# Transposed and split queries and keys made in the projection stage of a decoder-layer step on one Trainium2 core

## The chip, the core and the metric

The kernel runs on one core of a Trainium2 chip. A core has five engines that each work through a queue of their own, strictly in order: TensorE (PE: matmuls and transposes; PEld is its loading of the stationary operand), VectorE (DVE), ScalarE (ACT), GpSimd (POOL) and SyncE (SP, which here only issues DMAs). DMAs move data between the device memory and the core's SBUF; PE writes its results to PSUM banks, from which DVE and ACT read them. An instruction that waits for a semaphore holds up everything behind it on its engine. The metric is device time in microseconds (us) of one execution, lower is better.

## What is computed

One layer of a decoder for a prompt of 1024 rows and a decode batch of 8 rows that share the weights. Cut to what matters here:

```python
h = rmsnorm(x) @ w_in                      # q, k, v (8 heads of 64), f, u, z
logf = log_sigmoid(f + b_f)
# prompt, per head, causal:
c = cumsum(logf)
s = q @ k.T * 64 ** -0.5 + c[:, None] - c[None, :]
att = softmax(mask(s)) @ v
# decode rows: the same, against 8192 cached positions per row
x = x + concat(rmsnorm(att), rmsnorm(u * mixed(z))) @ w_o
x = x + cross_attention(x, 256 memory rows)
x = x + conv_gated_mlp(x)
return rmsnorm(x), k, v, logf, ...
```

Everything is fp32. A product is made from split operands: a value is written as a high part (rounded to the matmul's fp32r form) and a low part (the remainder), and three matmuls add high*high, high*low and low*high. `split` does this: ACT copies the high part, DVE subtracts it from the source to get the low part.

## The kernel before

**The prompt's stages** follow each other on PE: the projection by w_in (about 0 to 235 us of the profile, called p1 here), the attention of rows 0 to 511 (hf = 0, to about 355 us, mixed with the memory's keys and values), the attention of rows 512 to 1023 (hf = 1, to about 495 us), then w_o, cross-attention and the MLP of each half.

**p1** goes through five column groups: Q, then O_F (forget logits and u), K, V, Z. Each has 8 tiles of 128 rows, and a tile is 24 matmuls of 512 columns (48 of 260 in O_F). The first four Q tiles are computed together (`by_rows`). The weights come as four pieces per group on SP (L249), and each is split by ACT (wh, L235) and DVE (wl, L236). `evac` (L467) takes a tile out of PSUM with ACT (L469) and stores it with a DMA that ACT issues (L470): q to the scratch tensor q_d, k and v to the outputs.

**The decode batch** runs as a background program between the prompt's pieces. How many of its steps are issued is paced by the `yield` values of the prompt's code (table PACE): a stage with fewer or smaller yields gets fewer steps. A step on the cached keys multiplies a gathered 1 MB tile with the queries on DVE (L1444, 128x2048 in p1) and reduces it on DVE (L1448); within the attention the same work is cut into 128x512 pieces (L1435, L1436). GpSimd issues the gathers (L1428 keys, L1489 values), PE sums the values (L1495). The queries for this come by SP: `qs_d` is stored (L465) and read back as a broadcast row (L1398, tile d). Later the decode rows go through w_o, w_cq, the cached memory keys (cmk: L1680 multiplies, L1682 reduces, 16 pieces of each), whose scores PE transposes at L1687, the memory values, and the MLP.

**The attention** works per pair of heads (hp = 0 to 3). `load` fetches the pair's q, k and v from device memory in rows. `setup` makes the operands of the score matmuls: PE transposes four blocks of q (L750) and of k (L779); ACT copies the high parts of both heads (L757, L784, 64x512 each), DVE subtracts the low parts (L774, L788, 64x512 each), GpSimd copies the high part a second time (L758 for q, L785 for k), and GpSimd's DMAs add four rows that carry the cumulated logits. For hf = 0 GpSimd stores the finished k operands in ks_d (L791, L792); for hf = 1 SP reads them back (L769, L770) and only the second 512 keys are made anew. Then come for each block of 128 queries: scores on PE (L807, L809, L811), the row maximum on DVE (L813, L816), the exponential on ACT (L814, L817), transposes of the result on PE (L836), their copies by ACT or DVE (L843, L841), and the products with v on PE (L852). The setup of the next pair is run between the score blocks of the present one, at the places that LD and ST name.

**The order**: the code is written in the order of the stages, and a scheduler then puts each engine's instructions into one fixed queue, by its own estimate of when each could start. So a change in one place moves instructions of other parts in the queues; on the chip the queue is followed in order, whatever the true times are. Tiles come from rotating pools: `T2` has NT buffers of 128x512, `BA`, `BB` and `MS` are PSUM banks.

Of the kernel before, what the change touches and what calls it, by code (L numbers as in the profile page):

```python
# [7 lines left out]
F32 = mybir.dt.float32  # L8
# [52 lines left out]
LD = [(0, 1, 0), (0, 0, 0)]  # L61
ST = [(0, 1, 1), (0, 1, 1)]
# [5 lines left out]
NT = 7  # L68
# [3 lines left out]
SB = 2  # L72
# [6 lines left out]
def build(nc, tc, ctx, a, phases=None):  # L79
# [123 lines left out]
    q_d = dram.tile([T, AW], F32, tag="q_d", name="q_d")  # L203
# [6 lines left out]
    ks_d = dram.tile([NH, 64, 2, 512], F32, tag="ks_d", name="ks_d")  # L210
# [163 lines left out]
    def p1(early):  # L374
# [125 lines left out]
        for tt in range(8):  # L500
            ps, ps2 = BK(), BK()
            mm_chunk(tt, ws, ps[:, 0:260], 0, 260)
            mm_chunk(tt, ws, ps2[:, 0:260], 260, 260)
            if tt == SD - 1:
# [44 lines left out]
        for c0, dst in ((O_K, k_d), (O_V, v_d)):  # L549
            ws, sps = loaded(c0, 512, [(0, 512)])  # L550
            for tt in range(8):
                ps = BK()
                mm_chunk(tt, ws, ps, 0, 512)
                if tt == SD - 1:
# [15 lines left out]
                evac(ps, dst, rstd, tt)  # L570
# [155 lines left out]
    def attention(hf, queue, late=None, at=3):  # L726
# [3 lines left out]
        def load(hp):  # L730
            cs = slice(hp * P, (hp + 1) * P)
            qn = tpool.tile([P, 512], F32, tag="qn", bufs=1, name=nm("qn")).rearrange("p (i c) -> p i c", c=P)
            nc.sync.dma_start(qn, q_d[hf * 512 : (hf + 1) * 512, cs].rearrange("(i p) c -> p i c", p=P))
            if hf == 0:
                kvn = U([P, 2 * nk, P])
                kn, vn = kvn[:, :nk, :], kvn[:, nk:, :]
            else:
                kn, vn = T2().rearrange("p (i c) -> p i c", c=P), U([P, nk, P])
            nc.sync.dma_start(kn, k_d[hf * 512 : nk * P, cs].rearrange("(i p) c -> p i c", p=P))
            nc.sync.dma_start(vn, v_d[: nk * P, cs].rearrange("(i p) c -> p i c", p=P))  # L740
            return qn, kn, vn

        def setup(hp, qn, kn, vn):


            calm = lambda: tc.issue_after(lastexp[0]) if lastexp else nullcontext()
            with behind(ENG.PE):
                tr = BB() if hf else (MS, BB, BA)[SB]()
                for i in range(4):
                    nc.tensor.transpose(tr[:, i * P : (i + 1) * P], qn[:, i, :], ident)  # L750
            qab, ka, kb = [], [], []
            for j in range(2):
                h = hp * 2 + j
                rows = slice(64 * j, 64 * j + 64)
                qq = U([P, 2, 512], F32R)
                with calm():
# [1278 lines left out]
```

## Time and profile before

| | |
|---|---|
| three runs | 1790.96, 1792.46, 1794.57 us; median 1792.46 us |
| the profiled execution | 1791.7 us span, inside the range of the three runs |
| PE, DVE, ACT, POOL busy | 97%, 78%, 41%, 27% of the span |
| mean TensorE clock granted | 0.993 of full speed |
| DMA | 521.06 MB, 291 GB/s mean |

The profile has a page for the whole span and views for any stretch: windows (busy time of each engine), waits (who waited for whom), the timeline (one row per instruction or run of equal ones), the chain (the work that ended last, followed back) and the instructions of one line of the kernel. A row of the timeline gives start and duration in us, engine, line, operation, tiles, and in brackets how long the engine had been idle and what ended that. PE's matmuls are pipelined: one of 512 columns is shown with 0.39 us, and the next starts 0.23 us after it.

### The profile page before, as it was taken

The page shows a single profiled execution, that of the slowest core. Times are in us where ns is not written, and L with a number is a line of the kernel's source. Part 1 is how long each engine was busy: PE and PEld are TensorE (multiplying, and loading weights), DVE is VectorE, ACT ScalarE, POOL GpSimd, SP SyncE. Part 2 cuts the span into 40 slices and gives each one's busy share as a digit, 9 for nine tenths or more (in the row PEclk, how much of TensorE's full clock was granted, in tenths as well). Part 3 has the DMA queues.
Part 4 walks back from the last instruction along what each step waited for, and adds up shares of the span by engine and source line. Part 5 has one row for each costly group of instructions (what it writes and reads, how often), then busy time and mean ns, then how long its engine had stood idle before and what let it go on. Part 6 is the DMA issues. An engine that isn't in the chain of part 4 may idle for free.

```text
span 1791.7 us, 25124 instructions
## 1 busy us (share of the span) xinstructions
PE 1735.9 (97%) x9653; PEld 1285.7 (72%) x9653; DVE 1399.9 (78%) x1733; ACT 733.5 (41%) x1374; POOL 488.3 (27%) x461
## 2 busy tenths in 40 slices
PE   8999999889999999999999999999999999999997
PEld 5787777655677666767777777766666778768875
DVE  4689658989788986989999999898885549855344
ACT  6332355566643635333333244335353233333232
POOL 1252234443222332333322223433322112102110
PEclk9999999999999999999999999999999999999999
DMA  8786798777697975779788788988879587568982
GB/s 291 297 304 226 294 334 319 259 264 244 254 403 279 363 299 224 282 285 345 290 301 313 291 317 311 376 306 346 320 280 350 214 306 249 191 260 297 359 310 80
DMA packets 157074, 521.06 MB, mean 291 GB/s; under 512 B 20874, under 2 KB 40842, under 8 KB 124186
## 3 DMA queue, kind: packets, MB, share of 16 engines
q0 software_dynamic: 57168, 341.14, 50.0%
q1 hardware_dynamic: 92874, 165.73, 26.5%
q10 hardware_dynamic: 6912, 12.59, 1.9%
q8 instruction: 76, 1.25, 0.3%
q14 instruction: 44, 0.36, 0.1%
HBM read 495.47 MB, written 23.93 MB: 290 GB/s over the span
## 4 chain that ended last, share of the span: by engine, by line
PE 53%; issue 9%; DMA 8%; DVE 6%; ACT 2%; POOL 2%; POOLq 0%; DVEq 0%; ACTq 0%; SPq 0%
DMA kv<-cache_v,io 6%; PE ba L272 6%; PE ba L274 6%; PE ba L273 6%; PE dv L1495 4%; PE bb L272 3%; PE bb L273 3%; PE bb L274 3%; PE ba L1063 1%; DVE s L1448 1%; PE ba L1064 1%; PE ba L1065 1%; PE dv L331 1%; DMA kv<-cache_k,io 1%; PE dv L1774 1%
## 5 line engine op out<-in xcount | busy, mean ns | idle before, releaser
L235 ACT ACTIVATE wh<-wr 128x1024 fp32r<-128x1024 f32 (+2 forms) x220 | 228.6, 1044 | 443.3 <-PE ba L273 142.3
L236 DVE TENSOR_TENSOR wl<-wr,wh 128x1024 fp32r<-128x1024 f32 (+2 forms) x220 | 262.7, 1200 | 165.1 <-PE ba L274 57.4
L1428 POOL DMA_INDIRECT kv<-cache_k,io x128 | 186.9, 1460 | 606.8 <-DVE s L1448 327.2
L1444 DVE TENSOR_TENSOR kv<-kv,d 128x1024 f32<-128x1024 f32 (+1 forms) x156 | 258.0, 1681 | 32.6 <-DMA kv<-cache_k,io 32.6
L1448 DVE TENSOR_REDUCE s<-kv 128x16 f32<-128x1024 f32 (+1 forms) x156 | 258.4, 1672 | 0.0
L1489 POOL DMA_INDIRECT kv<-cache_v,io x128 | 160.8, 1256 | 239.4 <-PE dv L1495 155.2
L272 PE MATMUL ba<-u,wh 128*128 128x512 f32 x528 | 209.3, 397 | 0.0
L274 PE MATMUL ba<-u,wl 128*128 128x512 f32 x528 | 209.0, 396 | 0.0
L273 PE MATMUL ba<-u,wh 128*128 128x512 f32 x528 | 208.5, 395 | 0.5 <-DVE u L239 0.5
L272 PE MATMUL ba<-wh,u 128*128 128x512 f32 (+1 forms) x495 | 186.1, 379 | 0.9 <-ACT u L235 0.9
L273 PE MATMUL ba<-wl,u 128*128 128x512 f32 (+1 forms) x495 | 185.1, 375 | 1.3 <-DVE wl L236 1.3
L274 PE MATMUL ba<-wh,u 128*128 128x512 f32 (+1 forms) x495 | 183.4, 375 | 0.0
L1495 PE MATMUL dv<-kv,s 128*32 128x512 f32 x1024 | 127.1, 598 | 1.6 <-DMA kv<-cache_v,io 1.6
L274 PEld LDWEIGHTS ba<-u,wl 128*128 128x128 f32 x528 | 99.2, 188 | 29.0 <-issue 6.5
L272 PEld LDWEIGHTS ba<-u,wh 128*128 128x128 f32 x528 | 99.3, 188 | 26.4 <-issue 4.8
L273 PEld LDWEIGHTS ba<-u,wh 128*128 128x128 f32 x528 | 99.2, 188 | 25.2 <-issue 2.3
L272 PEld LDWEIGHTS ba<-wh,u 128*128 128x128 f32 x495 | 93.0, 188 | 25.0 <-issue 6.5
L272 PE MATMUL bb<-u,wh 128*128 128x512 f32 x272 | 108.7, 400 | 0.0
L274 PE MATMUL bb<-u,wl 128*128 128x512 f32 x272 | 108.0, 398 | 0.0
L273 PE MATMUL bb<-u,wh 128*128 128x512 f32 x272 | 107.9, 397 | 0.0
L273 PEld LDWEIGHTS ba<-wl,u 128*128 128x128 f32 x495 | 93.0, 188 | 20.1 <-DVE wl L236 1.9
L274 PEld LDWEIGHTS ba<-wh,u 128*128 128x128 f32 x495 | 92.9, 188 | 19.5 <-issue 1.6
(454 smaller groups left out, 3310.6 us busy)
## 6 DMA issues: line engine op xcount, KB each, us to landing
wr<-w_up SPq DMA_DIRECT2D x88, 512.0 KB
kv<-w_up POOLq DMA_DIRECT2D x22, 1024.0 KB
wr<-w_down SPq DMA_DIRECT2D x40, 512.0 KB
kv<-w_down POOLq DMA_DIRECT2D x11, 1024.0 KB
wr<-w_in SPq DMA_DIRECT2D x16, 512.0 KB
wr<-w_o SPq DMA_DIRECT2D x16, 512.0 KB
wr<-w_cq SPq DMA_DIRECT2D x16, 512.0 KB
wr<-w_co SPq DMA_DIRECT2D x16, 512.0 KB
```

Of the source, the lines that this page charges most:

```text
L235: nc.scalar.activation(h, src, AF.Copy)
L236: nc.vector.tensor_tensor(l, src, h.bitcast(F32), op=ALU.subtract)
L272: mmul(out, sh, mh, start=(i == 0), stop=False)
L273: mmul(out, sh, ml, start=False, stop=False)
L274: mmul(out, sl, mh, start=False, stop=(i == n - 1))
L331: mmul(ps[32 * j : 32 * j + 32, :w], xT[:, k, :] if nk == 8 else xT[:, k * 8 : k * 8 + 32], raw[:, q, j * w : (j + 1) * w], start=(k == 0) ...
L1063: mmul(pss[i], mh[k][:, tb], wh, start=(k == korder[0]), stop=False)
L1428: nc.gpsimd.indirect_dma_start(kv, None, a["cache_k"], off(kidx[:, b, ch : ch + 1]))
L1444: nc.vector.tensor_tensor(kvv[:, i : i + m, :], kvv[:, i : i + m, :], qb.unsqueeze(1).broadcast_to((P, m, 512)), op=ALU.mult)
L1448: nc.vector.tensor_reduce(s[:, ch * 4 + i : ch * 4 + i + m, :].rearrange("p k h -> p (k h)"), kvv[:, i : i + m, :].rearrange("p k (h d) -> ...
L1489: nc.gpsimd.indirect_dma_start(kv, None, a["cache_v"], off(kidx[:, b, ch : ch + 1]))
L1495: mmul(dv[32 * j : 32 * j + 32, :], s[:, ch * 4 : ch * 4 + 4, :].rearrange("p k h -> p (k h)"), kvv[:, j, :], start=(ch == 1), stop=(ch == ...
```

## The change

The queries and keys are transposed and split once, in p1, right behind the tile that makes them. `evac` hands its tile on, q is no longer stored in rows (q_d is gone), and each Q and K tile is put on a list, `flat`. `turn_over` takes entries from the list between later tiles: two after each of the Q tiles 4 to 7, one after each tile of O_F, K and V as long as there are any. An entry, `operand`, is four PE transposes, one split of 128x512 on ACT and DVE, and four DMAs of 128 KB that SP issues, to qt_d or kt_d (device memory, one 128x1024 block per head: 64 rows high part, 64 rows low part).

In the attention, `load` fetches the finished operands: v, qq (both parts in one transfer), ka and kb, on SP; GpSimd still copies the high parts a second time and still issues the DMAs for the logit rows. `setup` is gone with its transposes, copies and subtractions, and so are ks_d, its stores and re-loads, and the yields in between. NT goes from 7 to 8, and for hf = 1 the next pair is loaded one place later.

```diff
-LD = [(0, 1, 0), (0, 0, 0)]
-ST = [(0, 1, 1), (0, 1, 1)]
+LD = [(0, 1, 0), (0, 1, 0)]
-NT = 7
+NT = 8
         def evac(ps, dst, sc, tt):
             t = T2()
             nc.scalar.activation(t, ps, AF.Copy, scale=sc[:, tt : tt + 1])
-            nc.scalar.dma_start(dst[tt * P : (tt + 1) * P, :], t)
+            if dst is not None:
+                nc.scalar.dma_start(dst[tt * P : (tt + 1) * P, :], t)
+            return t
+        def operand(t, dst, tt):
+            tr = BK()
+            for hp in range(4):
+                nc.tensor.transpose(tr[:, hp * P : (hp + 1) * P], t[:, hp * P : (hp + 1) * P], ident)
+            h, l = T2(512, F32R), T2(512, F32R)
+            split(tr, h, l)
+            d = dst.rearrange("(hp j) (r d) t -> j r d hp t", j=2, r=2)
+            for r, src in enumerate((h, l)):
+                for j in range(2):
+                    nc.sync.dma_start(
+                        d[j, r][:, :, tt * P : (tt + 1) * P],
+                        src[64 * j : 64 * j + 64, :].bitcast(F32).rearrange("d (hp t) -> d hp t", t=P),
+                    )
+        def turn_over(n):
+            for _ in range(min(n, len(flat))):
+                flat.pop(0)()
                 mm_chunk(tt, ws, ps, 0, 512)
+                turn_over(2)
-            evac(ps, q_d, rstd8, tt)
+            flat.append(partial(operand, evac(ps, None, rstd8, tt), qt_d, tt))
...
-                with calm():
-                    nc.scalar.activation(qq[0:64, 0, :], tr[rows, :], AF.Copy)
+                nc.sync.dma_start(qq[:, 0, :].bitcast(F32), qt_d[h, :, s])
                 nc.gpsimd.tensor_copy(qq[0:64, 1, :], qq[0:64, 0, :].bitcast(F32))
...
+                nc.sync.dma_start(ka[j][0:64, :].bitcast(F32), kt_d[h, 0:64, : nk * P])
+                nc.gpsimd.tensor_copy(ka[j][64:128, :], ka[j][0:64, :].bitcast(F32))
+                nc.sync.dma_start(kb[j][0:64, :].bitcast(F32), kt_d[h, 64:128, : nk * P])
                 nc.gpsimd.dma_start(kb[j][64:68, :], ck_d[h, :, : nk * P])
...
                         if hp < 3 and (blk, j, ii) == LD[hf]:
-                            raw = load(hp + 1)
-                        if hp < 3 and (blk, j, ii) == ST[hf]:
-                            nxt = setup(hp + 1, *raw)
-                        if nxt:
-                            next(nxt, None)
-                            yield 1
+                            nxt = load(hp + 1)
```

Counted over the queues: PE's number of transposes and matmuls is the same (64 transposes leave the attention, 64 enter p1). ACT loses 32 copies of 64x512 and gets 16 of 128x512, and loses 8 DMA issues; it gets two more table loads. DVE loses 32 subtractions of 64x512 and gets 16 of 128x512. Of the 64 decode pieces of each kind in the attention (L1435, L1436) 12 move to later stages, where they run as larger ones. GpSimd loses 16 DMAs; its copies of k become 8 of 64x512 and 8 of 64x1024. SP issues 484 DMAs instead of 412: 8 loads of q rows, 8 of k rows and 24 of ks_d leave, 64 stores and 48 loads of the finished operands come.

The queues show where things moved. First DVE's queue where Q ends and O_F begins. Before, the four low parts of O_F's weights (wl, L236) stand ahead of the decode's first multiplications (L1444):

```order
L236 TENSOR_TENSOR wl_556<-wr_554,wh_557 128x1040
L236 TENSOR_TENSOR wl_566<-wr_564,wh_567 128x1040
L236 TENSOR_TENSOR wl_576<-wr_574,wh_577 128x1040
L236 TENSOR_TENSOR wl_586<-wr_584,wh_587 128x1040
L1444 TENSOR_TENSOR kv_348<-kv_348,d_61_345 128x2048
L1444 TENSOR_TENSOR kv_388<-kv_388,d_61_345 128x2048
L1444 TENSOR_TENSOR kv_453<-kv_453,d_61_345 128x2048
L1444 TENSOR_TENSOR kv_485<-kv_485,d_61_345 128x2048
```

In the changed kernel (its own line numbers: L234 is the subtraction of `split` and `wload`, L1419 and L1423 the decode's multiplication and reduction, L1383 a scan of the decode's logits; t are low parts of Q tiles) the same place reads, behind the low parts of Q tiles 0 to 3 and two multiplications:

```order
L1419 TENSOR_TENSOR kv_475<-kv_475,d_61_345 128x2048
L1419 TENSOR_TENSOR kv_532<-kv_532,d_61_345 128x2048
L1383 SCALAR_TENSOR_TENSOR d_157_1173<-rmask,d_157_1173 128x512
L1423 TENSOR_REDUCE s_347<-kv_348 128x32
L234 TENSOR_TENSOR t_90_569<-bb_563,t_89_568 128x512
L234 TENSOR_TENSOR t_93_582<-ba_576,t_92_581 128x512
L1423 TENSOR_REDUCE s_347<-kv_388 128x32
L234 TENSOR_TENSOR wl_639<-wr_637,wh_640 128x1040
L1423 TENSOR_REDUCE s_347<-kv_475 128x32
L234 TENSOR_TENSOR wl_649<-wr_647,wh_650 128x1040
L1383 SCALAR_TENSOR_TENSOR d_451_2679<-rmask,d_451_2679 128x512
L1423 TENSOR_REDUCE s_347<-kv_532 128x32
```

Behind these stand the third and fourth wl and the low parts of Q tiles 6 and 7. So all four multiplications, four reductions, two scans and the low parts of two Q tiles now stand ahead of O_F's last two low parts, of which before none did.

The second place is DVE's queue at the second setup of hf = 1. Before, between the row maxima (L816) and the decode's pieces (L1435, L1436):

```order
L774 TENSOR_TENSOR u_3543<-bb_3538,u_3543 64x512
L774 TENSOR_TENSOR u_3553<-bb_3538,u_3553 64x512
L1435 TENSOR_TENSOR kv_3527<-kv_3527,d_490_2860 128x512
L816 TENSOR_REDUCE mx_3668<-ba_3669 128x1
L1436 TENSOR_REDUCE s_2862<-kv_3527 128x8
L788 TENSOR_TENSOR u_3548<-bb_3595,u_3547 64x512
L788 TENSOR_TENSOR u_3558<-bb_3595,u_3557 64x512
L1435 TENSOR_TENSOR kv_3527<-kv_3527,d_490_2860 128x512
```

In the changed kernel (L803 is the row maximum, L1410 and L1411 the decode's pieces, L861 the scaling of the result) there are no subtractions:

```order
L1411 TENSOR_REDUCE s_3300<-kv_3557 128x8
L932 TENSOR_SCALAR u_2630<-u_2630,rar_3686 128x512
L803 TENSOR_REDUCE mx_3719<-ba_3720 128x1
L803 TENSOR_REDUCE mx_3766<-ba_3767 128x1
L861 TENSOR_TENSOR u_3701<-bb_3703,rl_3671 128x128 x2
L1410 TENSOR_TENSOR kv_3756<-kv_3756,d_615_3298 128x512
L850 RECIPROCAL rl_3820<-ls_3621 128x4
```

What moved here: the four subtractions are gone, and the maxima stand closer together.

The third place is the decode's stage on the cached memory keys, late in the program. Before, between the third and the fourth tile's multiplications (L1680) DVE's queue has six rows of the prompt's MLP, of which these end the stretch (L1307, L1308, L1310: convolution of a tile; L236: low part of a weight piece):

```order
L1682 TENSOR_REDUCE sS_12084<-kv_12246 128x4 x2
L236 TENSOR_TENSOR wl_12530<-wr_12528,wh_12531 128x1024
L1308 SCALAR_TENSOR_TENSOR t_2277_12283<-ba_12258,gp,t_2277_12283 128x510
L1310 TENSOR_TENSOR t_2277_12283<-t_2277_12283,fix_11178 128x2
L1680 TENSOR_TENSOR kv_12293<-kv_12293,d_2278_12289 128x2x512
L1680 TENSOR_TENSOR kv_12293<-kv_12293,d_2279_12290 128x2x512
```

In the changed kernel (L1655 and L1657 are those lines, L1282 the first part of the convolution) the fourth tile follows the third at once:

```order
L1655 TENSOR_TENSOR kv_12305<-kv_12305,d_2295_12301 128x2x512
L234 TENSOR_TENSOR wl_12585<-wr_12583,wh_12586 128x1024
L1655 TENSOR_TENSOR kv_12305<-kv_12305,d_2296_12302 128x2x512
L1655 TENSOR_TENSOR kv_12393<-kv_12393,d_2308_12389 128x2x512
L1657 TENSOR_REDUCE sS_12163<-kv_12215 128x4 x2
L1282 SCALAR_TENSOR_TENSOR t_2317_12436<-bb_12411,gp,t_2317_12436 128x511
L1655 TENSOR_TENSOR kv_12393<-kv_12393,d_2309_12390 128x2x512
```

What moved: the decode reaches this stage later and leaves it at the same point of the prompt. From the first multiplication to the last reduction DVE's queue has 72 rows before and 59 now, and PE's queue has 369 matmuls before and 287 now from the end of the decode's w_cq to L1687.

More of the change, by code (lines that the diff above doesn't have):

```diff
@@ L553, in p1 @@
                 mm_chunk(tt, ws, ps, 0, 512)
+                turn_over(1)
                 if tt == SD - 1:
@@ L731, in load @@
             cs = slice(hp * P, (hp + 1) * P)
[L732 to L739, printed above, removed]
-            nc.sync.dma_start(vn, v_d[: nk * P, cs].rearrange("(i p) c -> p i c", p=P))
[L741 to L750, printed above, removed]
+            vn = U([P, nk, P])
+            nc.sync.dma_start(vn, v_d[: nk * P, cs].rearrange("(i p) c -> p i c", p=P))
             qab, ka, kb = [], [], []
```

52 lines of the change are left out of this document (12 added, 40 removed).

## The prediction

> **What bounds the kernel now.** I read the page first, then the windows, then single stretches.
>
> ```profile
> span 1791.7 us, 25124 instructions
> PE 1735.9 (97%) x9653; PEld 1285.7 (72%) x9653; DVE 1399.9 (78%) x1733; ACT 733.5 (41%) x1374; POOL 488.3 (27%) x461
> ```
>
> TensorE (PE) is busy 97% of the span, and the change leaves its number of transposes and matmuls as it is. So the change cannot save PE work; it can only move it and change how long PE waits. The windows (start and end, length, then busy us of PE, PEld, DVE, ACT, POOL, granted clock, DMA share, GB/s) say where that could be:
>
> ```profile
> 25.00:50.00 25.00, 25.00 (x107) 19.43 (x106) 5.03 (x11) 16.05 (x28) 9.29 (x10) 1.00 0.98 381
> 50.00:75.00 25.00, 22.15 (x154) 17.84 (x153) 13.35 (x8) 9.92 (x13) 0.86 (x1) 1.00 0.84 315
> 75.00:100.00 25.00, 25.00 (x205) 24.15 (x204) 25.00 (x19) 5.95 (x11) 9.08 (x6) 1.00 0.68 251
> 350.00:375.00 25.00, 21.11 (x128) 14.69 (x125) 21.93 (x46) 18.08 (x52) 12.91 (x19) 0.80 0.81 264
> 375.00:400.00 25.00, 21.66 (x150) 14.48 (x148) 20.33 (x33) 15.53 (x36) 9.76 (x12) 0.99 0.66 211
> 400.00:425.00 25.00, 22.06 (x152) 14.06 (x150) 24.88 (x42) 15.53 (x31) 8.22 (x10) 1.00 0.69 239
> 500.00:600.00 100.00, 100.00 (x527) 77.31 (x525) 88.42 (x115) 40.15 (x84) 28.34 (x23) 1.00 0.91 342
> 1480.00:1550.00 70.00, 69.08 (x301) 55.87 (x300) 69.14 (x86) 25.66 (x43) 11.72 (x19) 1.00 0.71 241
> ```
>
> In the projection (p1) PE is full from 75 us on: what is added there, or held up there, is paid. In the attention (350 to 425) PE idles 3 to 4 us of each 25, DVE is 80 to 99% busy, and the clock dips once. From 500 on PE is full again, and at 1480 to 1550 PE and DVE are full together.
>
> **Term 1: p1, +26 us.** The added transposes are cheap. The rows of L750 give one; four follow each other in 0.45 us on the chain:
>
> ```profile
> L750 PE MATMUL bb<-cp,qn x16: 272/273/476, 357.5 to 444.0; 128*128 128x128 f32 x16
> 385.86 0.45 PE bb L750 x4
> ```
>
> 64 transposes are 16 x 0.45 = 7.2 us, half of them for Q and half for K. Their splits (16 on ACT, 16 on DVE) lie beside PE. What costs is DVE's order where Q ends and O_F begins. Its timeline before, and three of PE's rows there:
>
> ```profile
> 53.19 1.24 DVE L236 TENSOR_TENSOR wl<-wr,wh 128x1040 fp32r<-128x1040 f32 x1 [7.73 <-PE ba L273]
> 62.79 3.74 DVE L236 TENSOR_TENSOR wl<-wr,wh 128x1040 fp32r<-128x1040 f32 x3 [8.36 <-ACT wh L235]
> 66.45 8.89 DVE L1444 TENSOR_TENSOR kv<-kv,d 128x2048 f32<-128x2048 f32 x4
> 75.39 1.21 DVE L1408 TENSOR_TENSOR_SCAN d<-rmask,d 128x512 f32<-128x512 f32 x1
> 76.52 8.84 DVE L1448 TENSOR_REDUCE s<-kv 128x32 f32<-128x2048 f32 x4
> 62.25 0.39 PE L272 MATMUL ba<-wh,u 128*128 128x260 f32 x1
> 64.09 0.39 PE L273 MATMUL ba<-wl,u 128*128 128x260 f32 x1 [0.72 <-DVE wl L236]
> 66.58 0.39 PE L273 MATMUL ba<-wl,u 128*128 128x260 f32 x1 [0.35 <-DVE wl L236]
> ```
>
> PE starts O_F at 62.25 and takes each low weight part within half a microsecond of its making; the last one is ready at 66.5. In the changed queue the decode's four multiplications, its four reductions, two scans and two low parts of Q tiles stand ahead of that last part. The multiplications need the broadcast queries d, whose load SP issues late:
>
> ```profile
> 61.45 0.34 SPq L1398 DMA_DIRECT2D d<-qs_d  x1
> SPq L1398 <- DMA qs_d<-t: 23.3, 1, 23.3
> L236 DVE TENSOR_TENSOR u<-ba,u x10: 658/682/692, 617.8 to 1274.5; 128x512 fp32r<-128x512 f32 x10
> ```
>
> That load waited 23.3 us for the store of qs_d, behind weights on busy DMA engines. Without the q_d stores it may go a few us earlier. I let DVE start multiplying at 62.5 (bounds 60 and 66.5, the latter since the old DVE found it ready). Then 8.89 + 2 x 1.21 + 8.84 + 2 x 0.68 + four wl of 1.24 = 26.5 us, and the last wl is ready at 89.0 instead of 66.5: PE is 22.5 us late. 28 of the Q transposes lie inside this wait. The K transposes and the last four (36 x 0.11 = 4.0 us) come on top, since PE is full. Sum +26, between +20 (some of it caught up) and +30. The weights of K wait on SP behind Q's stores, but PE needs them only about 50 us after their old issue at 62.4, so this costs nothing unless the stores take longer than that.
>
> **Term 2: the attention, -24 us.** What vanishes there, per setup: eight transposes, four copies and four subtractions.
>
> ```profile
> L757 ACT ACTIVATE u<-bb x8: 587/592/597, 358.5 to 444.9; 64x512 fp32r<-64x512 f32 x8
> L774 DVE TENSOR_TENSOR u<-bb,u x8: 683/689/696, 361.5 to 446.8; 64x512 fp32r<-64x512 f32 x8
> L1435 DVE TENSOR_TENSOR kv<-kv,d x64: 656/681/1059, 269.9 to 493.0; 128x512 f32<-128x512 f32 x64
> 346.14 0.25 PE ba L750 x3
> 347.67 0.60 ACT u L757
> 396.67 0.59 DVE u L788
> 397.27 0.69 DVE u L788
> 397.96 0.60 DVE kv L1435
> 443.80 0.44 PE bb L750 x4
> ```
>
> The last six are pieces of the chain of waits. From 338 to 495 the chain holds 24 pieces of setup, first and last shown, that add up to 8.4 us, and 5.5 us of decode pieces (L1435, L1436), of which I count half, 2.8, as 12 of 64 move away. For hf = 0 32 transposes (3.5 us) leave a PE that is nearly full. That is 14.7 us directly. DVE is also relieved as a whole: 32 x 0.689 + 12 x (0.681 + 0.68) = 38 us less between 235 and 495, and ACT 32 x 0.59 = 19 us less. If the stretch shrank with DVE's work, it would lose 38 us. The lower bound is 7 us (PE's own transposes). Where DVE's queue is full, as at 400 to 425 (24.88 of 25), every maximum behind a subtraction gets earlier, so I go above the direct sum, to 24.
>
> The 12 pieces are three whole decode steps. They run later, in stages like 500 to 600, where PE has 100.00 of 100 and DVE 88.42: DVE has room for them beside PE, so 0. If it has none, they cost 3 x (2.2 + 2.2) = 13 us (by the rows of L1444 and L1448 above).
>
> GpSimd's second copies stay. Those of 64x1024 are not in the trace; between 0.61 (one of 64x512) and twice that I take 1.2 us.
>
> ```profile
> L758 POOL CAST u<-u x16: 600/624/1712, 241.4 to 449.1; 64x512 fp32r<-64x512 f32 x16
> POOL kv L1428 <- DVE s L1436: 44.5, 6, 16.1
> ```
>
> They stand in GpSimd's queue among gathers that wait up to 16.1 us for DVE, but are issued a pair ahead instead of just in time; I take 0, and 16 us for a handover at which this fails. One copy took 1.71 us instead of 0.60. [...]
>
> **Term 3: the cached memory keys, +7 us.** The decode reaches this stage later and leaves it at the same place in the prompt: PE's queue has 82 matmuls fewer in it, about 19 us at 0.23 us each (107 in 25 us, from 25 to 50). The 32 DVE operations of the stage stay:
>
> ```profile
> L1680 DVE TENSOR_TENSOR kv<-kv,d x16: 1212/1218/1224, 1479.9 to 1539.7; 128x1024 f32<-128x1024 f32 x16
> L1682 DVE TENSOR_REDUCE sS<-kv x16: 1204/1208/1220, 1485.1 to 1545.6; 128x4 f32<-128x1024 f32 x16
> ```
>
> Before, 69.1 us of each engine lie in 70. After, PE has 69 - 19 = 50 us, and DVE, which loses 13 of 72 rows of about half a microsecond, 62.6. PE's transpose at L1687 needs all of it, so PE waits up to 12.5 us; part of it can be made up by DVE rows that run later. I take 7, between 0 and 12.5.
>
> **Sum:** 26 - 24 + 7 = +9 on the profiled 1791.7 us, 1800.7. The median of the runs is 0.8 above this span, so 1801.5; I say 1801.
>
> **Rivals.**
> (a) *The wait in p1 does not arise* (DVE finds the decode's data early, or PE has other work): then p1 costs its transposes alone, 7 or 8 us, and 8 - 24 + 7 = -9 gives 1783.5 on the scale of the runs, faster. Against it: PE's and DVE's queues are fixed, and d was issued at 61.45. Chance 0.1.
> (b) *The attention shrinks with DVE's whole relief*: 26 - 38 + 5 = -7, 1785.5, faster. For it: DVE's 24.88 of 25. Against it: most of the chain there is PE's own. [...] Chance 0.17.
> (c) *The attention gives back only PE's transposes*, since the loop of scores, maximum, exponential and transposes closes behind the gap, or GpSimd's copies are late: 26 - 7 + 7 = +26, 1818.5, slower still. Chance 0.13.
> The forecast has 0.6, with a range of its own from 1794 to 1809.
>
> A difference of 0.2% (3.6 us) is about what a measurement of this kernel can tell from none. Slower by more: 0.52 of the forecast's 0.6 and all of (c), 0.65. Faster: most of (a) and (b), 0.2. Between: 0.15. The range from 1784 to 1817 cuts the outer parts of (a), (b) and (c).
>
> **What would show it.** Right: PE idle for some 20 us between 55 and 90 with "DVE wl" as releaser, the decode's multiplications ahead of it on DVE, and p1 ending about 26 us later; the attention shorter by 20 to 30 us, without setup on the chain; PE waiting at L1687 late in the span. Wrong: PE full from 62 us on; the attention as long as before, with GpSimd's copies or SP's loads as releasers of the scores; or PE waiting in later stages for the moved decode steps.

## The result, and the profile after

The changed kernel takes 1834.97 us (median of 4 runs, 1833.58 to 1836.37), the kernel before, on the same chip, 1791.71 us (4 runs). The ratio is 1.0224, with a 95% interval of 1.0201 to 1.0247: 43 us slower. The forecast said slower, by 9 us.

The page of the changed kernel (span, then busy us of each engine):

```profile
span 1833.6 us, 25147 instructions
PE 1751.0 (95%) x9653; PEld 1295.0 (71%) x9653; DVE 1387.9 (76%) x1703; ACT 727.5 (40%) x1360; POOL 470.5 (26%) x445
```

PE has the same 9653 instructions. The span grew by 41.9 us: PE idles 26.8 us more, and is busy 15.1 us more for the same work; the mean granted clock is 0.982 (0.993 before). DVE, ACT and POOL all have less to do. The windows of the changed kernel (columns as in the prediction; the seventh number is the granted clock) show where:

```profile
50.00:75.00 25.00, 15.74 (x93) 11.68 (x91) 14.66 (x10) 9.38 (x12) 1.56 (x2) 0.86 0.78 231
75.00:100.00 25.00, 19.49 (x121) 17.64 (x120) 19.31 (x14) 5.83 (x10) 7.32 (x3) 0.80 0.95 332
400.00:425.00 25.00, 21.86 (x158) 14.57 (x157) 19.42 (x35) 13.30 (x29) 10.16 (x13) 1.00 0.99 287
500.00:600.00 100.00, 93.14 (x474) 71.07 (x473) 80.42 (x102) 34.13 (x61) 29.65 (x21) 0.95 0.84 316
```

From 50 to 100 us PE is busy 35.2 us of 50 (47.2 before), and the granted clock is 0.86 and 0.80 where it was 1.00. From 500 to 600 PE had 100.00; now it has 93.14 at 0.95.

Three places of PE's queue divide the loss: the first score matmul (L807 before, L794 after), the first matmul by w_o (L1063, L1038), and the end. Groups of their lines, of before and of after (count, shortest/median/longest ns, then first and last start):

```profile
L807 PE MATMUL ba<-u,u x96: 221/412/616, 263.0 to 471.0; 128*128 128x384 f32 x24, 128*128 128x512 f32 x24, 128*128 128x320 f32 x16, 128*128 128x448 f32 x16
L1063 PE MATMUL ba<-wh,u x96: 387/394/797, 491.0 to 1296.0; 128*128 128x512 f32 x96
```

```profile
L794 PE MATMUL ba<-u,u x96: 222/393/795, 291.8 to 488.7; 128*128 128x384 f32 x24, 128*128 128x512 f32 x24, 128*128 128x320 f32 x16, 128*128 128x448 f32 x16
L1038 PE MATMUL ba<-wh,u x88: 387/394/801, 505.4 to 1325.2; 128*128 128x512 f32 x88
```

So p1 costs 28.8 us (263.0 to 291.8). The attention gains 14.4 (228.0 to 213.6). From 14.4 us late at w_o the kernel goes to 41.9 late at the end: **27.5 us are lost behind the attention**, where the prediction had 7.

**p1.** Seven of the waits of the changed kernel between 40 and 110 us (who waited for whom: us in total, times, longest):

```profile
ACT wh L233 <- DMA wr<-w_in: 10.8, 2, 10.3
DVE t L234 <- DMA qt_d<-t: 8.6, 1, 8.6
ACT t L467 <- DMA qt_d<-t: 8.2, 2, 5.2
PE ba L478 <- ACT t L467: 7.8, 1, 7.8
ACT t L315 <- DMA qt_d<-t: 6.2, 1, 6.2
PE bb L321 <- DVE fl L536: 2.8, 1, 2.8
PE bb L271 <- DVE wl L234: 0.9, 1, 0.9
```

PE's expected wait for wl (L271) is 0.9 us. Three other waits end with a store to qt_d that landed: DVE and ACT wanted a T2 buffer that a store still held. The timelines of SP, ACT, PE and DVE, one after another:

```profile
57.65 0.36 SPq L1373 DMA_DIRECT2D d<-qs_d  x1
58.10 10.07 SPq L484 DMA_DIRECT2D qt_d<-t  x14
...
80.32 6.85 SPq L247 DMA_DIRECT2D wr<-w_in  x4
```

```profile
61.83 0.69 ACT L467 ACTIVATE t<-ba,rstd 128x512 f32<-128x512 f32 x1 [5.15 <-DMA qt_d<-t]
...
92.95 1.06 ACT L233 ACTIVATE wh<-wr 128x1024 fp32r<-128x1024 f32 x1 [10.30 <-DMA wr<-w_in]
```

```profile
62.57 1.12 PE L478 MATMUL ba<-cp,t 128*128 128x128 f32 x4 [7.83 <-ACT t L467]
...
63.91 0.63 PE L271 MATMUL ba<-wl,u 128*128 128x512 f32 x1
...
65.57 0.40 PE L272 MATMUL ba<-wh,u 128*128 128x512 f32 x1
```

```profile
61.03 8.90 DVE L1419 TENSOR_TENSOR kv<-kv,d 128x2048 f32<-128x2048 f32 x4 [2.00 <-DMA d<-qs_d]
...
76.55 1.23 DVE L234 TENSOR_TENSOR wl<-wr,wh 128x1040 fp32r<-128x1040 f32 x1
...
84.35 2.38 DVE L234 TENSOR_TENSOR wl<-wr,wh 128x1040 fp32r<-128x1040 f32 x2
```

SP's queue explains the first: all but two of the early Q stores stand behind the load of d, which waits until 57.65 for qs_d. So the buffers of T2 stay held, ACT gets one for Q tile 5 only at 61.83, and PE, whose next instruction is the transposes of that tile, waits 7.83 us. Behind it PE is slow: 0.63 us for a matmul that takes 0.40 two microseconds later. DVE's order is as predicted (last wl ready at 86.7; 89.0 was forecast), but PE was already late. Then ACT stands 10.30 us before the weights of K, which SP could issue only at 80.32 behind the stores. O_F's evacuations stand behind that on ACT, and PE waits 2.8 us for a DVE row (fl, L536) that needs one of them.

**Behind the attention.** In the window from 560 to 580 of the changed kernel DVE is full and PE is not; DVE's and PE's timelines there:

```profile
560.00:580.00 20.00, 15.89 (x88) 12.96 (x89) 19.97 (x29) 5.05 (x13) 5.18 (x4) 0.83 0.47 158
```

```profile
556.43 2.35 DVE L1419 TENSOR_TENSOR kv<-kv,d 128x1024 f32<-128x1024 f32 x2
...
562.14 1.40 DVE L667 SCALAR_TENSOR_TENSOR u<-u,rz,xg 128x512 f32<-128x512 f32 x2
563.47 0.68 DVE L990 TENSOR_TENSOR u<-ba,u 128x512 f32<-128x512 f32 x1
```

```profile
564.21 0.48 PE L1099 MATMUL ba<-cp,u 128*128 128x128 f32 x1 [2.71 <-DVE u L990]
```

The same place before (L641 and L1015 are those lines):

```profile
533.31 2.33 DVE L1448 TENSOR_REDUCE s<-kv 128x16 f32<-128x1024 f32 x2
...
538.62 1.41 DVE L641 SCALAR_TENSOR_TENSOR u<-u,rz,xg 128x512 f32<-128x512 f32 x2
...
541.12 1.22 DVE L236 TENSOR_TENSOR wl<-wr,wh 128x1024 fp32r<-128x1024 f32 x1
542.26 0.68 DVE L1015 TENSOR_TENSOR u<-ba,u 128x512 f32<-128x512 f32 x1
```

Two decode multiplications, 2.35 us together, now end 4.7 us ahead of the row that PE needs (L990); before, the last decode rows ahead of it, two reductions of 2.33 us together, ended 6.6 us ahead. That these multiplications make the wait is argued, not shown. Behind PE's 2.71 us the granted clock is 0.50 from 565 to 570, which takes more. In 100 us DVE has room (80.42); in these 20 it has none. Over the whole stretch behind the attention PE idles 40.3 us (25.7 before): its waits for DVE grew from 3.8 to 10.6 us, those for ACT from 10.9 to 18.1.

### The profile page after: what moved, and what is told of

Same layout as the page of the kernel before. It is cut to its first block, busy times and chain, and to the rows that moved or that the text cites. A ratio compares the mean times of both kernels' runs of the same rounds, so it can differ in the third digit from the quotient of the medians.

```text
span 1833.6 us, 25147 instructions
## 1 busy us (share of the span) xinstructions
PE 1751.0 (95%) x9653; PEld 1295.0 (71%) x9653; DVE 1387.9 (76%) x1703; ACT 727.5 (40%) x1360; POOL 470.5 (26%) x445
## 4 chain that ended last, share of the span: by engine, by line
PE 75%; DVE 8%; DMA 5%; issue 4%; ACT 3%; POOL 1%; SPq 0%; DVEq 0%; POOLq 0%; ACTq 0%
PE ba L270 11%; PE ba L271 11%; PE ba L272 11%; PE bb L270 6%; PE bb L272 5%; PE bb L271 5%; PE dv L1470 5%; DVE wl L234 1%; PE dv L329 1%; PE dv L1749 1%; DVE kv L1419 1%; DMA kv<-cache_k,io 1%; DVE s L1423 1%; DMA u<-kt_d 1%; PE ms L839 1%
## 5 line engine op out<-in xcount | busy, mean ns | idle before, releaser
L234 DVE TENSOR_TENSOR wl<-wr,wh 128x1024 fp32r<-128x1024 f32 (+2 forms) x220 | 263.6, 1206 | 151.1 <-PE ba L272 48.5
L1403 POOL DMA_INDIRECT kv<-cache_k,io x128 | 163.1, 1274 | 633.6 <-DVE s L1423 386.5
L1419 DVE TENSOR_TENSOR kv<-kv,d 128x1024 f32<-128x1024 f32 (+1 forms) x161 | 265.2, 1674 | 34.7 <-DMA kv<-cache_k,io 32.7
L1423 DVE TENSOR_REDUCE s<-kv 128x16 f32<-128x1024 f32 (+1 forms) x161 | 265.4, 1665 | 0.3
L1464 POOL DMA_INDIRECT kv<-cache_v,io x128 | 173.5, 1355 | 297.6 <-PE dv L1470 215.1
L271 PE MATMUL ba<-u,wh 128*128 128x512 f32 x544 | 215.5, 396 | 2.8 <-DVE u L237 2.8
L270 PE MATMUL ba<-u,wh 128*128 128x512 f32 x544 | 216.5, 398 | 0.0
L270 PE MATMUL ba<-wh,u 128*128 128x512 f32 (+1 forms) x503 | 195.2, 389 | 4.5 <-ACT u L233 2.0
L271 PE MATMUL ba<-wl,u 128*128 128x512 f32 (+1 forms) x503 | 192.3, 383 | 0.0
L272 PE MATMUL ba<-wh,u 128*128 128x512 f32 (+1 forms) x503 | 190.1, 383 | 0.0
L271 PEld LDWEIGHTS ba<-u,wh 128*128 128x128 f32 x544 | 102.3, 188 | 32.0 <-issue 7.1
L272 PEld LDWEIGHTS ba<-u,wl 128*128 128x128 f32 x544 | 102.2, 188 | 28.8 <-issue 5.5
L270 PEld LDWEIGHTS ba<-wh,u 128*128 128x128 f32 x503 | 97.0, 193 | 30.0 <-issue 3.4
L272 PEld LDWEIGHTS ba<-wh,u 128*128 128x128 f32 x503 | 96.5, 192 | 23.0 <-issue 5.2
L271 PEld LDWEIGHTS ba<-wl,u 128*128 128x128 f32 x503 | 97.0, 193 | 18.2 <-issue 0.8
L270 PE MATMUL bb<-u,wh 128*128 128x512 f32 x256 | 101.6, 397 | 0.0
L272 PE MATMUL bb<-u,wl 128*128 128x512 f32 x256 | 101.5, 396 | 0.0
L271 PE MATMUL bb<-u,wh 128*128 128x512 f32 x256 | 101.3, 396 | 0.0
```

The source lines that it names most:

```text
L234: nc.vector.tensor_tensor(l, src, h.bitcast(F32), op=ALU.subtract)
L270: mmul(out, sh, mh, start=(i == 0), stop=False)
L271: mmul(out, sh, ml, start=False, stop=False)
L272: mmul(out, sl, mh, start=False, stop=(i == n - 1))
L1403: nc.gpsimd.indirect_dma_start(kv, None, a["cache_k"], off(kidx[:, b, ch : ch + 1]))
L1419: nc.vector.tensor_tensor(kvv[:, i : i + m, :], kvv[:, i : i + m, :], qb.unsqueeze(1).broadcast_to((P, m, 512)), op=ALU.mult)
```

## The experiments

All times are medians beside runs of the kernel before on the same chip; its medians there lie between 1789.7 and 1795.7 us, so runs from different chips are best compared by their ratios. "Late" is against before's profile: at the start of K (its sample matmuls, L306 at 111.8 before), at the first score (263.0), at the first w_o (491.0), and at the end (1791.7).

| run | us | ratio (95%) | K | score | w_o | end |
|---|---|---|---|---|---|---|
| the change | 1835.0 | 1.0201 to 1.0247 | 20.3 | 28.8 | 14.4 | 41.9 |
| q_only | 1821.2 | 1.0144 to 1.0204 | 21.1 | 20.9 | 17.8 | 22.0 |
| k_only | 1809.2 | 1.0075 to 1.0116 | -0.8 | 17.3 | 9.6 | 18.5 |
| wl_first | 1833.9 | 1.0212 to 1.0253 | 17.4 | 35.5 | 18.5 | 44.4 |
| paced | 1832.8 | 1.0196 to 1.0245 | 21.4 | 29.0 | 27.8 | 41.2 |
| parts_in_u | 1827.7 | 1.0155 to 1.0232 | 15.3 | 21.5 | 7.4 | 37.6 |
| parts_in_u_wl_first | 1824.8 | 1.0134 to 1.0219 | 14.8 | 20.0 | 6.9 | 31.7 |
| stores_on_act | 1861.6 | 1.0358 to 1.0427 | 24.1 | 42.1 | 30.4 | 67.7 |
| parts_in_u_act | 1836.0 | 1.0223 to 1.0306 | 21.2 | 26.8 | 12.4 | 41.8 |
| before_no_yields | 1820.0 | 1.0128 to 1.0191 | -1.5 | -1.5 | -7.8 | 25.8 |
| low_parts_first | 1833.7 | 1.0202 to 1.0268 | 1.1 | 23.4 | 8.9 | 39.4 |
| low_parts_first_paced | 1831.6 | 1.0184 to 1.0259 | 0.7 | 25.8 | 27.1 | 35.9 |
| k_only_parts_in_u | 1811.7 | 1.0080 to 1.0144 | -1.6 | 14.0 | 12.9 | 17.7 |
| k_late | 1828.9 | 1.0169 to 1.0212 | 0.5 | 9.3 | -4.9 | 36.5 |
| k_late_paced | 1814.6 | 1.0075 to 1.0199 | 0.7 | 7.9 | -1.4 | 16.9 |
| k_only_k_late | 1812.7 | 1.0083 to 1.0122 | -1.2 | 10.4 | 13.5 | 21.3 |
| low_parts_first_t2 | 1837.5 | 1.0193 to 1.0299 | 14.0 | 28.2 | 12.4 | 41.9 |
| k_late_more_yields | 1818.7 | 1.0091 to 1.0153 | 1.0 | 16.5 | 26.3 | 27.1 |
| before_more_yields | 1822.7 | 1.0139 to 1.0184 | -1.7 | -1.7 | 25.2 | 28.5 |

The last four columns come from one profile each. Kernels with the same p1 repeat the start of K within 1.7 us, but not always the first score: k_late, k_late_paced and k_late_more_yields have the same queues up to there and reach it 9.3, 7.9 and 16.5 us late. So a difference of less than some 9 us in that column is only a hint.

**The two halves apart.** q_only keeps before's k_d, ks_d and setup for the keys; k_only keeps q_d and setup for the queries (NT = 7).

```diff
 # q_only, against the change
-                if c0 == O_K:
-                    flat.append(partial(operand, t, kt_d, tt))
...
 # k_only, against the change
-            flat.append(partial(operand, evac(ps, None, rstd8, tt), qt_d, tt))
+            evac(ps, q_d, rstd8, tt)
...
```

> The change for the queries alone: Q tiles are transposed, split and stored in p1 and the attention loads them ready made; the keys are handled as in the kernel before (rows, setup with four transposes, copies, subtractions, and the yield of the setup). Theory A (the loss in p1 comes from the Q operands: decode's work ahead of O_F's last wl, evacuations that wait for buffers held by the Q stores, late weights of K): nearly all of p1's loss stays, the first score is 20 to 27 us later than before (28.8 with the whole change), and the whole kernel is 20 to 40 us slower than before. Rival B (the loss in p1 comes from the added work and traffic of both, or of the K part): the first score is at most 15 us later and the kernel within 10 us of before.

> The change for the keys alone: K tiles are transposed, split and stored in p1 and loaded ready made; the queries are stored in rows and set up in the attention as before, with the setup's yield. Theory A: p1 loses little more than the K transposes, 3 to 8 us, the attention gains, and the kernel is between 15 us faster and 5 us slower than before. Rival B: p1 loses 13 us or more, and the kernel is slower by over 10 us.

The queries behave as theory A has it (score 20.9 late). The keys do not: 17.3 us late instead of 3 to 8, all of it lost behind the start of K (-0.8 there). So p1 has two separate losses, and rival B is right for the second.

**DVE's order alone.**

```diff
+            if not opened[0]:
+                later.append(work)      # the decode's multiplications and reductions
+                return 1
...
         ws, sps = loaded(O_F, 520, [(8, 512), (0, 8)])
+        opened[0] = True
+        with tc.issue_after(newest(ENG.DVE)):
+            while later:
+                later.pop(0)()
...
```

> The changed kernel, but the decode's first multiplications are held back in DVE's queue until O_F's four low weight parts (wl) have been queued, the place they had before. Theory A1 (p1's loss is DVE's order, as the prediction had it): PE's wait for wl near 65 to 90 us goes, O_F ends 15 to 20 us earlier than in the changed kernel, and the kernel gains 15 to 22 us on it. Rival A2 (the Q stores on SP and the weights of K that wait behind them set the pace, DVE's order is only one of several holds of the same length): PE still waits behind ACT for evacuations and for the weights of K, p1 gains at most 10 us on the changed kernel.

Three of 20.3 us come back at the start of K, the first score is 6.7 us later than in the change, and the end does not move: A2. DVE's order by itself, the main mechanism of the prediction, does not set the time.

**The ring of T2.**

```diff
-            h, l = T2(512, F32R), T2(512, F32R)
+            hl = U([P, 2, 512], F32R)
+            h, l = hl[:, 0, :], hl[:, 1, :]
```

> The changed kernel, but the high and low part that an operand is split into lie in one buffer of the U pool instead of two of the eight T2 buffers, so T2 holds only the tiles that are evacuated. Theory E (p1's loss is the ring of T2: three of eight buffers per operand, held until stores land that stand on SP behind the load of d, so that evacuations on ACT wait for a buffer and PE waits for them): the waits of ACT and DVE for the Q stores (8.6 + 8.2 + 6.2 us between 40 and 110 us in the changed kernel) fall below 5 us together, PE's 7.8 us wait ahead of the transposes goes, the first score comes 10 us or more earlier than in the changed kernel, and the kernel is 8 to 25 us faster than the changed one. Rival F (the decode's work on DVE and the late weights of K set the end of the Q and O_F stage, with whatever buffers): the first score moves by less than 6 us and the time by less than 8 us.

> As the run before (parts in the U pool), and the decode's first multiplications held back until O_F's four wl are queued on DVE. Theory E with DVE's order as the second hold that then shows (both must be lifted): 10 us or more faster than the parts in the U pool alone, p1's loss against before at most 12 us, and the whole kernel within 15 us of before. Rival: the order of DVE costs nothing even then, within 4 us of the run with the parts in the U pool alone.

PE's 7.8 us wait is gone, but only 5 us come back at the start of K, and 7.3 at the first score, between what theory E and rival F had expected. Adding wl first gives 0.5 at the start of K. PE and DVE of parts_in_u_wl_first show what holds now:

```profile
83.61 0.58 PE L270 MATMUL bb<-wh,u 128*128 128x260 f32 x1 [9.46 <-DVE u L234]
```

```profile
57.95 4.00 DVE L234 TENSOR_TENSOR wl<-wr,wh 128x1040 fp32r<-128x1040 f32 x3 [0.20 <-PE ba L271]
61.87 8.89 DVE L1426 TENSOR_TENSOR kv<-kv,d 128x2048 f32<-128x2048 f32 x4
...
76.32 6.64 DVE L1430 TENSOR_REDUCE s<-kv 128x32 f32<-128x2048 f32 x3
82.88 0.68 DVE L234 TENSOR_TENSOR u<-bb,u 128x512 fp32r<-128x512 f32 x1
```

The wl are ready at 62, but low parts of Q tiles (u) stand behind the decode, and each holds the PSUM bank that PE needs for its next tile. The next run puts those ahead of the decode too; low_parts_first_t2 does so with the parts back in T2.

```diff
             turn_over(1)
+            if tt == 0:                 # O_F's first tile
+                turn_over(8)
+                opened[0] = True
+                ...
```

> The changed kernel with the parts in the U pool, and the decode's first multiplications held back on DVE until both O_F's wl and the low parts of all Q tiles are queued. Theory I (the DVE order of the prediction is a cause, but for two reasons: wl stand behind the decode and, once they do not, the low parts of the Q tiles do, which hold the PSUM bank that PE needs next): PE's wait of 9.5 us for a low part goes, p1's idle time falls from 21.6 us (parts in U, wl first) to 11 to 14, against 10.1 before, and the first score is at most 12 us later than before. Rival J (the decode's first steps only move the hold to the next group): the first score is still 17 us or more later than before.

> Low parts first, but with the parts in T2 as in the changed kernel. This tells the ring of T2 from DVE's order in the stage of Q and O_F (20.3 us late at the first matmul of K in the changed kernel, 15.3 with the parts in U, 17.4 with wl first, 1.1 with both and the low parts first). If the ring alone is enough to hold that stage, it stays 10 us or more late; if DVE's order is the whole cause, it is within 5 us of before.

The stage of Q and O_F is back to 1.1 us late; with the parts in T2 it is 14.0. So the ring (14.0) and DVE's order (15.3, parts_in_u) each hold this stage when the other is lifted, side by side: that is why lifting one gave so little. The late weights of K hold little here: in low_parts_first SP issues them at 81.70, later than in the change.

```profile
81.70 2.63 SPq L247 DMA_DIRECT2D wr<-w_in  x4
```

But the first score is still 23.4 us late, as rival J has it: the loss reappears in the K stage.

**The stores on ACT.** `nc.scalar.dma_start` for the 64 stores, with the parts in T2 and in U:

> The changed kernel with the 64 stores of the operands issued by ACT instead of SP, so that they do not stand behind SP's load of d and do not stand ahead of the weights of K. Theory E2 (the buffers are held because SP's queue holds the stores): stores land within a few us, the waits for them go, the weights of K are issued near 65 instead of 80 us, and p1 gains 10 us or more on the changed kernel. Rival E3 (the stores are slow by themselves, since the DMA engines are full of weights and gathers): the waits for stores stay as long, p1 gains less than 5 us or loses, as ACT's queue now waits for DVE's low parts as well.

> Parts in the U pool and the stores on ACT together. Theory E with E2: at least as fast as the better of the two alone, the first score at most 15 us later than before. Rival E3: no faster than the parts in the U pool alone, by 4 us or more slower where ACT waits for low parts.

Both misses for theories E and E2: 27 us slower than the change, and 8 slower than the parts in U alone. The times are as rival E3 had them, but ACT's longest hold there is not a wait for low parts. ACT, DVE and again ACT of parts_in_u_act:

```profile
46.98 12.97 ACTq L485 DMA_DIRECT2D qt_d<-u  x8
47.59 0.68 DVE L234 TENSOR_TENSOR u<-ba,u 128x512 fp32r<-128x512 f32 x1
60.33 1.84 ACT L467 ACTIVATE t<-ba,rstd 128x512 f32<-128x512 f32 x3 [12.89 <-DMA qt_d<-u]
```

DVE has both low parts ready at 48.3, and still the eight stores take ACT's queue until 59.95, with three evacuations behind them. What holds the stores there stays open.

**The K stage.** The keys alone, with the parts in U:

> The change for the keys alone, with the parts in the U pool. Theory E (the ring of T2 is what holds the K stage: ACT waited 8.2 us for a buffer and PE 9.6 us behind it): that wait goes, the first score comes 7 to 12 us earlier than with the keys alone in T2 (17.3 us late), and the kernel is at most 10 us slower than before. Rival F: the first score moves by less than 4 us.

Only 3 us of p1 come back (rival F, though a difference of this size is within the scatter named above). SP, DVE and PE of low_parts_first in that stage:

```profile
129.68 6.31 SPq L485 DMA_DIRECT2D kt_d<-u  x3
...
147.38 0.28 SPq L551 DMA_DIRECT2D o_lfs<-lfs  x1
...
150.67 0.23 SPq L553 DMA_DIRECT2D lfz<-o_lfs  x1
```

```profile
153.64 0.24 DVE L1396 TENSOR_TENSOR tot<-d,lfz 128x8 f32<-128x8 f32 x2 [6.25 <-DMA lfz<-o_lfs]
```

```profile
153.86 0.60 PE L1401 MATMUL ms<-tot,cp 128*128 128x8 f32 x2 [5.67 <-DVE tot L1396]
```

The decode's small load of lfz waits on SP behind K's stores, and a matmul of 8 columns holds PE 5.67 us. To test it, K's operands are moved behind that load:

```diff
-                turn_over(1)
+                turn_over((2 if tt > 3 else 0) if c0 == O_K else 1)
```

> As low parts first (parts in U, decode's first multiplications behind wl and Q's low parts), and the operands of K start only with K tile 4, two behind each tile, so that SP's stores of them stand behind the decode's small store and load (o_lfs, lfz) instead of ahead. Theory K (p1's loss in the K stage is SP's queue: K's stores, which wait for splits, stand ahead of the load of lfz, DVE waits 6 to 7 us for lfz and PE 6 us for DVE): the wait of PE at the decode's ms<-tot goes, the K stage loses less than 8 us where it lost 22, and the first score is 6 to 14 us later than before (7 of them the transposes). Rival L (the decode is simply late there, whatever SP does): the first score stays 18 us or more late.

> The change for the keys alone, parts in U, operands of K from tile 4 on. Theory K: the first score is at most 8 us later than before (14.0 with the keys alone and parts in U), and the kernel at most 12 us slower than before. Rival L: no gain on the keys alone with the parts in U, within 4 us of it.

In k_late the first score is 9.3 us late, of which the transposes' own time is 7.2, and the wait at ms<-tot is gone, as theory K has it; from the start of K 8.8 us are lost, a little more than the 8 it allowed. Little of this reaches the end: k_late loses 41.4 us behind the attention, where the change loses 27.5, and ends 36.5 late. The same edit on the keys alone gave 3.6 us of 14.0 and no time: too little to tell K from L there, and what is left of that kernel's p1 loss stays open (a wait of 5.2 us for an evacuation on ACT is the largest). In k_late the transposes of K start later as well, so SP's order and the later start are not told apart. SP's order can be only a part: the load of lfz, behind stores of the logit rows too, is issued 2.4 us earlier than in low_parts_first.

```profile
148.25 0.25 SPq L553 DMA_DIRECT2D lfz<-o_lfs  x1
```

**The decode's pace.** `paced` puts yields back into the changed attention (64 pieces of each kind there, as before, instead of 52):

```diff
                             nxt = load(hp + 1)
+                        if hp < 3 and (blk, j, ii) >= (0, 1, 1):
+                            yield 1
```

> The changed kernel with yields put back in the attention at the places where the setup used to yield, so that the decode gets as many steps there as before. Theory C (the losses behind 505 us, +10 to 600 us, +5 to 1460 us and +10 in the stage of the cached memory keys, are the 12 decode pieces that moved out of the attention and the decode's lag): these 15 to 25 us shrink by half or more; the attention itself may get up to 10 us longer; the kernel is 5 to 20 us faster than the changed one. Rival D (the later losses are something else, such as the prompt's own order): the later losses stay, and the kernel is as slow as the changed one or slower by what the attention loses.

The loss behind the attention halves (27.5 to 13.4), as theory C has it, but the attention's gain goes with it (14.4 to 1.2), and the time stays, as rival D has it. The mirror image takes the yield out of the kernel **before**, with nothing else changed, so that the same 52 pieces run there:

```diff
                             next(nxt, None)
-                            yield 1
```

> The kernel before, with one line taken out: the yield of 1 that follows each piece of a setup in the attention. Nothing of the queries or keys changes; the decode just gets fewer steps in the attention, as in the changed kernel, and runs them later. Theory G (it is the moved decode steps that make the changed kernel's attention shorter, and the same steps that cost it time behind the attention): the attention (first score to first w_o) gets 8 to 14 us shorter than before's 228, and the stages behind it lose 12 to 25 us, so that the whole kernel is 2 to 15 us slower than before. Rival H (the changed attention is shorter because setup's copies and subtractions are gone, and the later losses come from elsewhere): the attention shortens by less than 4 us, the stages behind it lose less than 4 us, and the time is within 4 us of before.

Rival H is out. The attention gets 6.3 us shorter, and 33.6 us are lost behind it, more than theory G had allowed: 29 us slower for a missing yield. Its waits of PE between 510 and 1330 us are many, and none of them is longer than 4.3 us; the first three:

```profile
PE dv L1494 <- DMA kv<-cache_v,io: 5.6, 2, 4.3
PE ba L280 <- ACT u L238: 3.6, 4, 2.4
PE bb L281 <- DVE wl L236: 2.4, 3, 1.0
```

The other direction, `yield 2` in the kernel before (76 pieces):

> The kernel before with the setup's yields at 2 instead of 1: 76 decode pieces of each kind in the attention. If the price of a decode step is simply lower in the attention than behind it, it is 5 to 25 us faster than before (taking 12 out cost 29 us). If 64 is the balance, it is within 5 us of before or slower by up to 15 us.

27 us slower too, beyond the 15 allowed, but now the attention takes 26.9 us longer and the rest 3.3. So of 52, 64 and 76 pieces 64 is the best, and 12 pieces either way cost about two thirds of what the whole change costs. The same pace on the p1 repairs:

> As the run of low parts first, with the yields put back in the attention. Theory G: the stage of the cached memory keys loses less than 5 us (10 in the changed kernel), the attention is within 4 us of before, and the whole kernel is faster than without these yields by 0 to 12 us, as the steps are paid at either place. Rival H: no later loss goes, and it is slower than without the yields by what the attention loses.

> The same with the yields put back in the attention. If theories G, I and K hold together, p1 loses 6 to 14 us, the attention 0 to 4 less than before's 228, the stages behind 4 to 14, and the whole kernel is 8 to 22 us slower than before instead of 43: the mechanisms then account for the larger part of the loss. Rival: still over 30 us slower, which would mean that a mechanism is missing.

> As K late and paced, with yields of 2 instead of 1 in the attention, so that 76 decode pieces of each kind run there (64 before, 52 in the changed kernel). Theory M (the 16 to 19 us that K late and paced still loses behind the attention are the decode's lag, since its first steps start later in p1): the attention gets 4 to 8 us longer, the stages behind it 8 to 20 us shorter, and the whole is 4 to 12 us faster than K late and paced, within 16 us of before. Rival N (the rest of the loss is not the number of steps; 64 is where attention and the later stages balance): as slow as K late and paced or up to 10 us slower.

Without the repair of K's part the yields give 2 us (1833.7 to 1831.6), inside the noise. With p1 repaired they give 14 (1828.9 to 1814.6), but the four runs of k_late_paced spread from 1805.7 to 1829.7 us, and the intervals of the ratios overlap; the stage of the cached memory keys loses less than 1 us. k_late_paced and k_late_more_yields are the best forms of the whole change, 20 and 23 us slower than before; their ratios (1.0137 and 1.0122) cannot be told apart, so more yields do not help (rival N).

Of k_late_paced's 16.9 us in the profile p1 has 7.9; the attention gains 9.3 (0 to 4 expected), and 18.3 are lost behind it (4 to 14 expected). With 76 pieces the loss behind the attention is 0.8 us, but the attention is 9.8 longer than before instead of 9.3 shorter: 12 pieces more there cost 19.1 us and save 17.5 behind it. Either way some 10 us are lost behind p1 (9.0 and 10.6), and why stays open. NT and the later place of `load` were not varied alone. No kernel here beats the one before.

## Why the prediction failed, step by step

- **Term 1, p1, +26 (20 to 30): 28.8.** The size holds, the mechanism only in part. DVE's order came as forecast: multiplications from 61.0 (62.5), last wl at 86.7 (89.0). But the ring of T2 was not in the sum, and holds the same stage as long; lifting DVE's order alone gained nothing. The row that the term rested on, PE waiting for wl, is 0.9 us long, so it is partly luck that the size came out.
- **"The weights of K wait on SP behind Q's stores ... so this costs nothing":** the reservation attached to it came true. SP issued them at 80.32 instead of 62.43, and ACT stood 10.30 us before them with O_F's evacuations behind. It is a small hold: PE waits 2.8 us for it, and in low_parts_first, where they are issued at 81.70, K starts only 1.1 us late.
- **K's part of p1, 4.0 us of transposes:** the keys alone lose 17.3 us. What K's operands hold up besides was not counted; starting them from K tile 4 on brings 14 us back in k_late (of 23.4), through SP's order or the later start.
- **Term 2, the attention, -24 (7 to 38): -14.4.** The step that failed is the addition for DVE's relief above the direct 14.7. The transposes' 7.2 and the 6.3 that before_no_yields gains by moving the decode alone make 13.5; that would leave about 1 us for ACT's and DVE's copies and subtractions. This split adds numbers of different kernels and is argued, not shown: with the decode's pieces put back the gain is 1.2 in paced and 9.3 in k_late_paced. Rival (b) is out.
- **"DVE has room for them beside PE, so 0" (worst 13).** This is the step by which the range was missed: the changed kernel loses 27.5 us behind the attention, 20.5 more than the sum had. The same 12 pieces moved in the kernel before, with nothing else changed, lose 33.6 there, and put back in paced they halve the loss. A mean of 88 in 100 said nothing about short stretches like 560 to 580, where DVE is full and PE waits for it, and nothing about the waits for ACT, which grew by as much.
- **Term 3, the cached memory keys, +7 (0 to 12.5):** between the matmul of before's 1460.1 and the transpose at L1687 the delay grows from 31.3 to 41.1 us, 9.8. In this stretch PE also runs 448 matmuls instead of 392, since the decode's w_cq now stands behind the first mark, so the stage's own loss is less than 9.8. The size holds; with the pace restored it is 0.8 (390 matmuls). Not as forecast, PE waits only 0.4 us at L1687 itself; 4.1 us of waits for ACT's high parts (u) lie ahead of it.
- **GpSimd's copies and SP's loads in the attention, 0:** no wait of PE there names a copy, and only 0.9 us a load from kt_d.
- The sum: 26 - 24 + 7 = 9 was forecast; the places give 28.8 - 14.4 + 27.5 = 41.9.

## What to carry to other kernels

Code that is taken out takes its yields with it: count what they issued, and price those steps by the short stretches into which they fall, not by an engine's mean over 100 us. Here the cheapest way to learn their price was to take the one yield out of the old kernel. Before costing a moved store at nothing, list for its queue what stands ahead and behind, and for its buffer pool who needs the next buffer: here SP's order (d, then the stores), T2's eight buffers and DVE's order held the stage of Q and O_F side by side. Where removing one hold gains little, look for a second that ends at the same time before dropping the theory; here only both together gave the stage back.

## What the hardware showed

Behind two of its waits PE lost more than their length. Of the 41.9 us, 15.1 are PE busy longer with the same 9653 instructions, at a mean granted clock of 0.982 (0.993 before). Behind the 7.83 us wait, with PE's restart at 62.57, the granted clock is 0.50 from 60 to 65 and a matmul of 512 columns takes 0.63 us; at 65.19 one takes 0.55, and from 65.57, 3.0 us after the restart, they take 0.40. In the 20 us around the 2.71 us wait that begins at 561.5, with a wait of 0.80 us shortly ahead of it, the granted clock is 0.83, and from 565 to 570 it is 0.50. The prediction priced waits at their length. That the waits lower the clock is read from this order of events; no run shows it apart.
